# Expert stage of an encoder layer: TensorE in source order, residual ahead of the scatter, norm vectors in expert 14

## The chip, the cores and the metric

The kernel runs on one core of a Trainium2 chip. The metric is the device time of one execution in microseconds, the median of several runs. The engines of the core work side by side: TensorE (PE, matmuls), VectorE (DVE), ScalarE (ACT), GpSimd (POOL) and SyncE (SP), which issues the DMAs here.

## The reference, cut to what matters

```python
h = layer_norm(ALPHA * h + mix, ln1_g, ln1_b)           # 512 tokens x 1024; before it: attention and convolution
affinity = softmax(h @ w_router)                        # 16 experts
gates, idx = top_k(affinity.T, 64)                      # each expert picks its 64 best tokens
xg = h[idx]                                             # gather
a, u = xg @ w_gate[e], xg @ w_up[e]                     # 64x1024 by 1024x2048, for each expert e
y = (silu(a) * u) @ w_down[e] * gates                   # 64x2048 by 2048x1024
moe = zeros(512, 1024).at[idx].add(y)                   # scatter
out = layer_norm(ALPHA * h + moe, ln2_g, ln2_b)
```

All is float32. Each expert has three matrices of 8 MB, 403 MB for all 16; they are read once.

## The kernel before

**Stages.** Up to about 277 us the layer's first half runs (projections, attention, convolution, first norm, router, ranks of the first two experts). Then comes the expert stage, a loop over e = 0 to 15, two experts to a pair. An expert is a gate half (k = 0), an up half (k = 1), four steps j each, and a down part of eight chunks c. A step (k, j) reads one 2 MB transfer: two chunks of 128 rows by 2048 columns. In it run four inner steps (x, y): x is the chunk, y the 512-column bank, and each makes two matmuls, g = 0 and 1, on 64 of the 128 columns of TensorE. The trace shows every float32 matmul as two records, so an inner step is four records, a step (k, j) sixteen.

**Weights.** `stream` (L128) issues the next transfer on SP into the buffer at the front of `ring`, ten buffers `b0` to `b9` of 2 MB, and puts that buffer at the back; `take_big` takes one out for other use (for good with `back=False`). 22 chunks are fetched ahead, into the buffers under their other names `s_...` and a few small tiles. `stream` is called once behind each step (k, j) and each second down chunk, so a transfer can start when TensorE has read the buffer's last content.

**What rides along.** `ranks(e + 2)` (L1136): per token block a transpose of affinities, compares on VectorE (`mask`, L240), counts on TensorE (L245). `gather` (L1029): for each block of 128 columns four matmuls (L1044) and a ScalarE copy into `xg`, in expert 0 between the gate matmuls, for later pairs in the down part of each odd expert. `choice` (L1049): transposes and gates of the pair. `scatter` (L1083): for each token block t and half h two matmuls into one of two PSUM banks `sg`, from where the result goes into the sums `acc`; it runs in the up half of each even expert and, `alone`, in expert 15. `norm_rows` (L1116): the second norm of all rows without expert 15's. `spread` (L1006): turns a vector of 1024 numbers, kept as columns, into equal rows on all 128 partitions, by transposes and ScalarE copies.

**The residual.** `acc` takes a buffer in expert 2. The scatter of pair 0 writes it by a copy (L1097, L1099), the later ones add (L1095). `residual_pieces` (L1015), called from expert 3's first step on, takes a second buffer for a while; GpSimd makes eight pieces of alpha*h1 there, two operations each (L1024, L1025), and VectorE adds each to `acc` (L1027). The vectors of the second norm, `gb2`, are spread in expert 15, in the middle of its gate and up halves.

**What sets the order.** A scheduler orders the instructions of each engine by its own simulated times, but where the source calls `tc.keep_in_program_order`. The helper `tensor(...)` (L211) does that for a matmul as long as TensorE is in the set `ordered`; before, the expert stage calls `nc.tensor` directly and nothing there is pinned. Each engine runs its own instructions strictly in order. The gate and up results stand in `pgu`, one two-bank PSUM tile for each half:

```python
pgu = [ps.tile([128, 2, 512], F32, name=f"gu{k}") for k in range(2)]
...
nc.vector.tensor_tensor(hh[:, x], sg[:, x], p[:, x], op=OP.mult)   # behind the last up step, x = 0 and 1
...
nc.scalar.activation(sg, pgu[0], AF.Silu)                          # behind the last gate step
```

Of the kernel before, what the change touches and what calls it, by code (L numbers as in the profile page):

```python
# [46 lines left out]
def layer_kernel(ctx, tc, x, positions, emb_ln_g, emb_ln_b, w_in, q_norm_g, w_qb, kv_norm_g, w_kvb,  # L47
                 conv_w, conv_b, conv_ln_g, conv_ln_b, w_o, ln1_g, ln1_b, w_router,
                 w_gate, w_up, w_down, ln2_g, ln2_b, rope_rows, out):
    nc = tc.nc  # L50
# [949 lines left out]

    acc = []
# [4 lines left out]
    def spread(dst, c0, scale):  # L1006

        for q in range(2):
            p = ps.tile([128, 512], F32, name="sg", bufs=2)
            for c in range(4):  # L1010
                cc = c0 + 4 * q + c
                nc.tensor.transpose(p[:, c * 128:(c + 1) * 128], gb[:, cc:cc + 1].to_broadcast([128, 128]), ident)
# [36 lines left out]
    def choice(pair):  # L1049
# [9 lines left out]
        for x, src in enumerate((oh, turned)):  # L1059
            p = ps.tile([128, 512], F32, name="sg", bufs=2)  # L1060
            for t in range(TT):
                nc.tensor.transpose(p[:, t * 128:(t + 1) * 128], src[:, t], ident)
            g.append(quarter_tile(x, F32R))
            nc.scalar.activation(g[x], p, AF.Identity)
            for t in range(TT):
                nc.tensor.matmul(pg[:, 2 * x:2 * x + 2], src[:, t], aff[:, t, 2 * pair:2 * pair + 2],  # L1066
                                 start=t == 0, stop=t == TT - 1)
# [15 lines left out]
    def scatter(pair, alone):  # L1083

        g, _ = chosen.pop(pair)
        for t in range(TT):
            pp = [ps.tile([128, 512], F32, name="sg", bufs=2) for _ in range(2)]
            ts = slice(t * 128, (t + 1) * 128)
            for k, h in [(k, h) for k in range(2) for h in range(2)] if alone else [(k, h) for h in range(2) for k in range(2)]:
                rs = slice(h * 64, (h + 1) * 64) if alone else slice(0, 128)  # L1090
                nc.tensor.matmul(pp[h], g[h][rs, ts], parts[h][k][rs, :], start=k == 0, stop=k == 1)  # L1091
# [11 lines left out]
    def last_rows():  # L1103
# [3 lines left out]
        for hf in range(2):  # L1107
            for t in range(TT):
                nc.tensor.matmul(p[hf * 64:(hf + 1) * 64, :2], hot[E // 2 - 1][:, t, CAP:], ag[:, t],
                                 start=t == 0, stop=t == TT - 1)  # L1110
# [47 lines left out]
    for e in range(E):  # L1158
        pair, s = divmod(e, 2)
        last = e == E - 1  # L1160
        pgu = [ps.tile([128, 2, 512], F32, name=f"gu{k}") for k in range(2)]
# [14 lines left out]
        for k, j in order:  # L1176
# [4 lines left out]
            if last and (k, j) == (1, 0):  # L1181

                py = ps.tile([128, 512], F32, name="py")
                for t in range(TT):
                    for hf in range(2):
                        nc.tensor.matmul(py[hf * 64:(hf + 1) * 64], hot[E // 2 - 1][:, t, CAP:],
                                         acc[t][:, hf * 512:(hf + 1) * 512], start=t == 0, stop=False)
# [150 lines left out]
```

## Time and profile before

| what | us |
|---|---|
| median of 3 runs | 1203.52 (1202.52 to 1205.8) |
| profiled execution | 1208.29 |
| its span, first to last instruction | 1206.3 |
| TensorE busy (matmuls) | 1119.5 |
| VectorE, ScalarE, GpSimd busy | 400.4, 249.6, 203.2 |

The queues moved 422.85 MB in the span. Busy time is summed over the span; a record's time is from its start to its modelled end, so matmuls that run two at a time count once in the sum and each in the mean. The granted clock of TensorE is 1.00 (2.4 GHz) in nearly all of the expert stage.

### The profile page before, as it was taken

Reading aid. Unit: us, or ns where it says so; the run is one execution under the profiler, and the core shown is the slowest. Engines: PE = TensorE matmul, PEld = TensorE weight load, DVE = VectorE, ACT = ScalarE, POOL = GpSimd, SP = SyncE. Lnnn points to the kernel's source line nnn. Section 1 sums busy time; section 2 is a strip of 40 time slices with the busy share of each in tenths; the row PEclk is TensorE's granted clock in tenths of the full one; section 3 lists DMA queues with packets and bytes.
Section 4 is the critical chain, followed back from the end, with each engine's and each line's share of the span. In section 5 each row is a group of like instructions: output and inputs, shape, how many; then the busy total and the mean of one; then the engine's idle time right before and its main releaser. Section 6 shows DMA issues by size and latency. Waiting matters only on the chain.

```text
span 1206.3 us, 13663 instructions
## 1 busy us (share of the span) xinstructions
PE 1119.5 (93%) x5573; PEld 545.0 (45%) x5573; DVE 400.4 (33%) x905; ACT 249.6 (21%) x448; POOL 203.2 (17%) x234
## 2 busy tenths in 40 slices
PE   5899998999999998999999999999998998899996
PEld 3687776785334343433343334334332433243432
DVE  6799898543011115122021112011210122011252
ACT  4546677321111111101010011001000101010120
POOL 6778467210000007000000000000000000000041
PEclk9899899999999999999999999999999999999999
DMA  6421014777999998999999999999999999999996
GB/s 200 135 84 36 6 71 144 271 268 281 420 429 428 428 393 343 427 430 427 426 427 428 428 426 430 427 426 429 426 428 429 426 428 426 429 426 427 428 427 253
DMA packets 43681, 422.85 MB, mean 351 GB/s; under 512 B 5178, under 2 KB 13187, under 8 KB 18018
## 3 DMA queue, kind: packets, MB, share of 16 engines
q1 hardware_dynamic: 42032, 421.28, 84.3%
q8 instruction: 44, 0.72, 0.2%
q10 hardware_dynamic: 1506, 0.43, 0.2%
q0 software_dynamic: 80, 0.26, 0.1%
q14 instruction: 19, 0.16, 0.0%
HBM read 419.60 MB, written 2.36 MB: 350 GB/s over the span
## 4 chain that ended last, share of the span: by engine, by line
PE 73%; DMA 16%; DVE 6%; ACT 2%; issue 1%; POOL 1%; POOLq 0%; SPq 0%; ACTq 0%; DVEq 0%
PE gu L1199 30%; PE py L1276 16%; DMA b<-in_w_up_dram 6%; PE sg L1044 5%; DMA b<-in_w_down_dram 4%; PE pj L258 4%; PE pj L259 3%; PE pj L260 3%; DMA b<-in_w_gate_dram 3%; PE sg L1091 3%; PE st L772 1%; DVE sq L1210 1%; PE tr L1066 1%; DVE cv L453 1%; DMA s<-in_w_in_dram 1%
## 5 line engine op out<-in xcount | busy, mean ns | idle before, releaser
L1199 PE MATMUL gu<-b,xg 128*64 128x512 f32 x1920 | 439.1, 598 | 22.1 <-DVE sq L1210 10.9
L1199 PEld LDWEIGHTS gu<-b,xg 128*64 128x64 f32 x1920 | 133.8, 137 | 291.1 <-issue 244.5
L1276 PE MATMUL py<-b,sq 128*64 128x512 f32 x976 | 224.1, 598 | 0.0
L1056 POOL COPY sq<-oh 128x256 f32<-128x256 f32 x16 | 5.9, 400 | 799.4 <-PE sg L1250 799.4
L1210 DVE TENSOR_TENSOR sq<-sq,gu 128x512 f32<-128x512 f32 x30 | 20.6, 687 | 292.6 <-PE gu L1199 276.8
L1276 PEld LDWEIGHTS py<-b,sq 128*64 128x64 f32 x976 | 67.3, 136 | 109.4 <-issue 102.2
L258 PE MATMUL pj<-s,s 128*128 128x512 f32 x189 | 78.4, 424 | 7.6 <-ACT q L435 3.2
L1044 PE MATMUL sg<-oh,h 128*128 128x128 f32 x512 | 72.6, 290 | 8.3 <-DVE oh L1035 6.9
L1045 ACT ACTIVATE xg<-sg,gbp 128x128 f32<-128x128 f32 x64 | 29.3, 457 | 237.6 <-PE sg L1044 145.9
L1044 PEld LDWEIGHTS sg<-oh,h 128*128 128x128 f32 x512 | 64.6, 198 | 29.6 <-issue 21.6
L259 PE MATMUL pj<-s,s 128*128 128x512 f32 x189 | 77.1, 408 | 0.0
L228 POOL TENSOR_TENSOR s<-s,s 128x512 fp32r<-128x512 f32 (+2 forms) x54 | 64.8, 1223 | 19.0 <-ACT s L227 12.2
L240 DVE SCALAR_TENSOR_TENSOR mask<-tr,aff,ones_b 128x128 bf16<-128x128 f32 x84 | 26.1, 348 | 120.7 <-PE tr L238 120.7
L260 PE MATMUL pj<-s,s 128*128 128x512 f32 x157 | 63.2, 406 | 0.0
L453 DVE SCALAR_TENSOR_TENSOR cv<-s,q,cv 128x512 f32<-128x512 f32 x83 | 62.2, 749 | 1.7
L1212 ACT ACTIVATE sq<-gu 128x1024 f32<-128x1024 f32 x16 | 16.4, 1024 | 217.9 <-PE gu L1199 217.9
L1095 DVE TENSOR_TENSOR b<-sg,b 128x512 f32<-128x512 f32 x56 | 37.0, 687 | 58.3 <-PE sg L1091 58.3
L1091 PE MATMUL sg<-q,q 128*128 128x512 f32 (+1 forms) x128 | 42.2, 437 | 7.0 <-DVE b L1095 5.9
L1080 ACT ACTIVATE q<-py,gates 64x512 fp32r<-64x512 f32 x30 | 20.5, 682 | 131.7 <-PE py L1276 119.0
L258 PEld LDWEIGHTS pj<-s,s 128*128 128x128 f32 x189 | 37.5, 200 | 16.8 <-ACT q L435 3.7
L1081 DVE SCALAR_TENSOR_TENSOR q<-py,gates,q 64x512 fp32r<-64x512 f32 x30 | 22.5, 748 | 65.2 <-ACT q L1080 65.0
L259 PEld LDWEIGHTS pj<-s,s 128*128 128x128 f32 x189 | 37.4, 198 | 7.1
(288 smaller groups left out, 1112.8 us busy)
## 6 DMA issues: line engine op xcount, KB each, us to landing
b<-in_w_down_dram SPq DMA_DIRECT2D x60, 2048.0 KB, 25.8
b<-in_w_gate_dram SPq DMA_DIRECT2D x60, 2048.0 KB, 27.5
b<-in_w_up_dram SPq DMA_DIRECT2D x60, 2048.0 KB, 28.0
s<-in_w_gate_dram SPq DMA_DIRECT2D x8, 1024.0 KB, 6.8
s<-in_w_in_dram SPq DMA_DIRECT2D x12, 512.0 KB, 5.2
s<-in_w_up_dram SPq DMA_DIRECT2D x6, 1024.0 KB, 7.1
s<-in_w_down_dram SPq DMA_DIRECT2D x6, 1024.0 KB, 11.6
s<-in_w_o_dram SPq DMA_DIRECT2D x4, 1024.0 KB, 7.1
```

The costliest lines, as they stand in the source:

```text
L228: pin(eng, eng.tensor_tensor(lo, src, hi.bitcast(F32), op=OP.subtract))
L258: tensor(nc.tensor.matmul(p, a[0], b[0], start=start, stop=False, **kw))
L259: tensor(nc.tensor.matmul(p, a[0], b[1], start=False, stop=False, **kw))
L260: tensor(nc.tensor.matmul(p, a[1], b[0], start=False, stop=stop, **kw))
L453: nc.vector.scalar_tensor_tensor(part if k < CW - 1 else cva[j], src[k], w[k], cva[j] if k == n_act else part, op0=OP.mult, op1=OP.add)
L1044: nc.tensor.matmul(here, rows, oh[:, t, :], start=t == 0, stop=t == TT - 1)
L1045: nc.scalar.activation(xg[:, cc, :], here, AF.Identity, scale=gbp[:, 0, cc:cc + 1], bias=gbp[:, 1, cc:cc + 1])
L1091: nc.tensor.matmul(pp[h], g[h][rs, ts], parts[h][k][rs, :], start=k == 0, stop=k == 1)
L1095: nc.vector.tensor_tensor(a, pp[h], a, op=OP.add)
L1199: nc.tensor.matmul(p[g * 64:(g + 1) * 64, b, :], xg[:, c, s * CAP:(s + 1) * CAP], ws[a][2 * b + g], start=c == 0, stop=c == DC - 1)
L1210: nc.vector.tensor_tensor(hh[:, x], sg[:, x], p[:, x], op=OP.mult)
L1276: nc.tensor.matmul(py[x * 64:(x + 1) * 64, :], hT2[:, b, j, g * 64:(g + 1) * 64], w[2 * a + hf], start=f == 0 and not last, stop=f == 15)
```

## The change

1. TensorE joins `ordered` ahead of the expert stage and every matmul and transpose there goes through `tensor(...)`: its order is that of the source.
2. The rank steps stand behind every second inner step (`y` is 1) of the gate half, the last expert's scatter likewise.
3. `pgu` is four one-bank tiles; Silu is two operations.
4. `acc` is taken one step earlier, behind (2, 0, 0), the residual's buffer behind (2, 0, 1) in place of (3, 0, 0). GpSimd writes the residual straight into `acc`; every scatter, pair 0's too, adds to it. VectorE's eight adds (L1027) go.
5. `gb2` takes its buffer behind step (14, 0, 0), for good, and its spreads stand behind (14, 0, 0) and (14, 0, 1).

```diff
@@ ahead of the expert stage
+    ordered.add(nc.tensor)
     acc = []
@@ residual_pieces
         for a in range(2):
             spread(gb_l[a], a * DC, ALPHA)
+            yield
         for i in range(2 * TT):
             t, cs = i // 2, slice(i % 2 * 512, (i % 2 + 1) * 512)
-            r = t4[:, 2048 + i % 4 * 512:2048 + (i % 4 + 1) * 512]
+            r = acc[t][:, cs]
             nc.gpsimd.tensor_tensor(r, h1[:, t, cs], gb_l[0][:, cs], op=OP.mult)
             nc.gpsimd.tensor_tensor(r, r, gb_l[1][:, cs], op=OP.add)
-            yield
-            nc.vector.tensor_tensor(acc[t][:, cs], acc[t][:, cs], r, op=OP.add)
@@ gather, and likewise every other matmul and transpose of the stage
-                    nc.tensor.matmul(here, rows, oh[:, t, :], start=t == 0, stop=t == TT - 1)
+                    tensor(nc.tensor.matmul(here, rows, oh[:, t, :], start=t == 0, stop=t == TT - 1))
@@ scatter
                 if k == 1:
                     a = acc[t][:, h * 512:(h + 1) * 512]
-                    if pair:
-                        nc.vector.tensor_tensor(a, pp[h], a, op=OP.add)
-                    elif h:
-                        nc.vector.tensor_copy(a, pp[h])
-                    else:
-                        nc.scalar.activation(a, pp[h], AF.Identity)
+                    nc.vector.tensor_tensor(a, pp[h], a, op=OP.add)
@@ loop over the experts
-        pgu = [ps.tile([128, 2, 512], F32, name=f"gu{k}") for k in range(2)]
+        pgu = [[ps.tile([128, 512], F32, name=f"gu{k}{b}") for b in range(2)] for k in range(2)]
...
-                    if (k == 0) == last and not final and left > (0 if last else 1):
+                    if last:
+                        if k == 0 and y and left:
+                            step(sc)
+                            left -= 1
+                    elif k and not final and left > 1:
                         step(sc)
                         left -= 1
-                    elif k == 0:
+                    elif k == 0 and y:
                         step(rk)
...
-                nc.scalar.activation(sg, pgu[0], AF.Silu)
-            if residual is not None:
+                for b in range(2):
+                    nc.scalar.activation(sg[:, b], pgu[0][b], AF.Silu)
+            if (e, k, j) == (2, 0, 2):
                 step(residual)
                 step(residual)
             if last and (k, j) == (0, DC // 2 - 1):
-                gb2 = take_big()
...
                 nr = norm_rows()
...
-                if (e, k, j) == (2, 0, 2):
+                if (e, k, j) == (2, 0, 0):
                     t4 = take_big(back=False)
                     acc.extend(t4[:, t * D:(t + 1) * D] for t in range(TT))
-                elif (e, k, j) == (3, 0, 0):
+                elif (e, k, j) == (2, 0, 1):
                     residual = residual_pieces()
                     step(residual)
+                elif (e, k, j) == (E - 2, 0, 0):
+                    gb2 = take_big(back=False)
+                    g2, b2 = gb2[:, :D], gb2[:, D:2 * D]
+                    gb2h = quarters(gb2[:, 2 * D:])[:2]
+                    spread(g2, 2 * DC, 1.0)
+                elif (e, k, j) == (E - 2, 0, 1):
+                    spread(b2, 3 * DC, 1.0)
...
+                    stream(next_chunk[0] + 2)
```

TensorE at the end of expert 0, before. `s_...`, `sq` and `q_...` hold expert 0's weights, `b_...` expert 1's; `gu_2456` and `gu_2457` are expert 0's gate and up, `gu_2705` expert 1's gate.

```order
L1199 MATMUL gu_2456<-s_2420,xg 64x512 x4
L1199 MATMUL gu_2457<-sq,xg 64x512
L1199 MATMUL gu_2457<-q_2437,xg 64x512
L1199 MATMUL gu_2457<-q_2438,xg 64x512
L1199 MATMUL gu_2705<-b_2513,xg 64x512 x8
L1199 MATMUL gu_2705<-b_2541,xg 64x512 x5
L1199 MATMUL gu_2457<-sq,xg 64x512 x2
L1199 MATMUL gu_2457<-q_2439,xg 64x512
L1199 MATMUL gu_2457<-q_2440,xg 64x512
L1250 MATMUL tr<-ident,sq 128x128 x4
L1199 MATMUL gu_2705<-b_2541,xg 64x512 x3
L1199 MATMUL gu_2705<-b_2551,xg 64x512 x8
```

The same place after (`gu_2456` to `gu_2459` are expert 0's four banks):

```order
L1044 MATMUL sg<-oh,h_88 128x128 x4
L1194 MATMUL gu_2456<-s_2420,xg 64x512 x2
L1194 MATMUL gu_2457<-s_2420,xg 64x512 x2
L1194 MATMUL gu_2458<-sq,xg 64x512 x2
L1194 MATMUL gu_2458<-q_2437,xg 64x512
L1194 MATMUL gu_2458<-q_2438,xg 64x512
L1194 MATMUL gu_2459<-sq,xg 64x512 x2
L1194 MATMUL gu_2459<-q_2439,xg 64x512
L1194 MATMUL gu_2459<-q_2440,xg 64x512
L1253 MATMUL tr<-ident,sq 128x128 x4
L1253 MATMUL sg<-ident,sq 128x128 x4
L1279 MATMUL py<-s_2422,sq 64x512 x4
```

Expert 1's gate matmuls no longer stand among expert 0's; each gate pair stands right behind the gather of its column block, and the down matmuls (`py`) follow at once.

The queue of SP in expert 2 and 3, after. `b4` is the buffer that the residual's vectors were in (`b3` is `acc`):

```order
L157 DMA b5_2584<-in_w_down_dram 128x4096
L157 DMA b6_2607<-in_w_down_dram 128x4096
L157 DMA b7_2660<-in_w_gate_dram 128x4096
L157 DMA b4_2574<-in_w_up_dram 128x4096
L157 DMA b8_2681<-in_w_gate_dram 128x4096
L157 DMA b9_2693<-in_w_gate_dram 128x4096
```

In the ring `b4` stands behind `b2`; the scheduler has put its transfer ahead of that into `b8`.

The end of the queue of SP, before:

```order
L157 DMA b7_2657<-in_w_down_dram 128x4096
L157 DMA b8_2678<-in_w_down_dram 128x4096
L155 DMA b0_2503<-in_w_down_dram 128x1024 x4
L1133 DMA out_0_dram<-h1_88 128x1024 x4
```

And after (the last pair goes in four pieces in both):

```order
L157 DMA b8_2681<-in_w_down_dram 128x4096
L1128 DMA out_0_dram<-h1_88 128x1024
L157 DMA b9_2693<-in_w_down_dram 128x4096
L157 DMA b0_2489<-in_w_down_dram 128x4096
L1128 DMA out_0_dram<-h1_88 128x1024
L155 DMA b1_2499<-in_w_down_dram 128x1024 x4
L1128 DMA out_0_dram<-h1_88 128x1024 x2
```

Two of the four output transfers have moved ahead of the last down pairs.

## Rows read from the trace of the kernel before

**Rows 1.** The page: busy us, share, count; GB/s in 40 slices of 30.2 us.
```profile
PE 1119.5 (93%) x5573; PEld 545.0 (45%) x5573; DVE 400.4 (33%) x905; ACT 249.6 (21%) x448; POOL 203.2 (17%) x234
...
GB/s 200 135 84 36 6 71 144 271 268 281 420 429 428 428 393 343 427 430 427 426 427 428 428 426 430 427 426 429 426 428 429 426 428 426 429 426 427 428 427 253
```

**Rows 2.** Windows: busy us of each engine, granted clock, DMA share, GB/s.
```profile
290.00:330.00 40.00, 39.74 (x198) 15.83 (x194) 2.88 (x12) 4.73 (x7) 0.00 (x0) 1.00 0.99 415
420.00:485.00 65.00, 61.46 (x296) 23.83 (x294) 21.93 (x39) 7.54 (x12) 22.84 (x18) 0.97 0.93 371
485.00:950.00 465.00, 438.49 (x2200) 178.54 (x2198) 82.59 (x265) 45.71 (x77) 2.97 (x8) 1.00 1.01 428
950.00:1190.00 240.00, 223.45 (x1072) 88.65 (x1070) 56.79 (x107) 28.55 (x45) 16.74 (x16) 1.00 1.01 427
```

**Rows 3.** DMA issues of 490:560, then of 850:1150: count, KB, us to landing.
```profile
b<-in_w_gate_dram SPq DMA_DIRECT2D x4, 2048.0 KB, 17.6
...
b<-in_w_gate_dram SPq DMA_DIRECT2D x20, 2048.0 KB, 39.3
```

**Rows 4.** Time line, queue of SP: start us, us, what; two single issues.
```profile
288.48 0.33 SPq L157 DMA_DIRECT2D b<-in_w_down_dram  x1
...
319.42 0.33 SPq L157 DMA_DIRECT2D b<-in_w_down_dram  x1
```

**Rows 5.** Time line, TensorE, expert 0: start us, us, what, matmul records.
```profile
278.22 2.15 PE L1044 MATMUL sg<-oh,h 128*128 128x128 f32 x16 [0.26 <-DVE oh L1035]
...
324.27 6.23 PE L1199 MATMUL gu<-b,xg 128*64 128x512 f32 x28
```

**Rows 6.** Chain of work, two stretches: start us, us, what.
```profile
619.50 0.47 ACT xg L1045
...
621.22 3.58 PE py L1276 x16
...
624.81 0.26 PE tr L245 x7
...
663.91 0.98 PE tr L1066 x8
...
666.76 0.59 PE sg L1062 x4
```

**Rows 7.** Time line, GpSimd, then VectorE, while the residual is made.
```profile
454.55 5.02 POOL L1024 TENSOR_TENSOR b<-h,b 128x512 f32<-128x512 f32 x4 [20.41 <-ACT q L1080]
...
465.09 3.45 POOL L1024 TENSOR_TENSOR b<-h,b 128x512 f32<-128x512 f32 x2 [0.63 <-DVE both L249]
...
472.05 5.84 POOL L1025 TENSOR_TENSOR b<-b 128x512 f32<-128x512 f32 x4
...
454.56 0.76 DVE L1081 SCALAR_TENSOR_TENSOR q<-py,gates,q 64x512 fp32r<-64x512 f32 x1 [1.54 <-ACT q L1080]
...
461.43 3.58 DVE L1027 TENSOR_TENSOR b<-b,b 128x512 f32<-128x512 f32 x1
```

**Rows 8.** Chain of work, then TensorE, in the last expert.
```profile
1101.73 36.06 DMA b<-in_w_gate_dram
...
1149.79 37.42 DMA b<-in_w_down_dram
...
1184.01 13.95 PE L1276 MATMUL py<-b,sq 128*64 128x512 f32 x64
```

**Rows 9.** TensorE by line, 1137 to 1206: count, busy us, mean ns.
```profile
L1091 PE MATMUL sg<-q,q 64*128 64x512 f32 x16 | 5.1, 444 | 0.8 <-DVE b L1095 0.8
...
L1012 PE MATMUL sg<-ident,gb 128*128 128x128 f32 x16 | 2.4, 282 | 0.0
```

**Rows 10.** Waits: engine, line, whom; us in total, times, longest.
```profile
PE gu L1199 <- DVE sq L1210: 10.9, 13, 0.9
...
PE tr L245 <- DVE mask L240: 7.2, 7, 1.3
...
PE sg L1091 <- DVE b L1095: 5.9, 13, 0.8
```

More of the change, by code (lines that the diff above doesn't have):

```diff
@@ L1065, in choice @@
             for t in range(TT):
-                nc.tensor.matmul(pg[:, 2 * x:2 * x + 2], src[:, t], aff[:, t, 2 * pair:2 * pair + 2],
-                                 start=t == 0, stop=t == TT - 1)
+                tensor(nc.tensor.matmul(pg[:, 2 * x:2 * x + 2], src[:, t], aff[:, t, 2 * pair:2 * pair + 2],
+                                 start=t == 0, stop=t == TT - 1))
             yield
@@ L1090, in scatter @@
                 rs = slice(h * 64, (h + 1) * 64) if alone else slice(0, 128)
[L1091 removed]
+                tensor(nc.tensor.matmul(pp[h], g[h][rs, ts], parts[h][k][rs, :], start=k == 0, stop=k == 1))
                 if k == 1:
                     a = acc[t][:, h * 512:(h + 1) * 512]
[L1094 to L1099 removed]
+                    nc.vector.tensor_tensor(a, pp[h], a, op=OP.add)
                     if h or not alone:
@@ L1108, in last_rows @@
             for t in range(TT):
-                nc.tensor.matmul(p[hf * 64:(hf + 1) * 64, :2], hot[E // 2 - 1][:, t, CAP:], ag[:, t],
-                                 start=t == 0, stop=t == TT - 1)
+                tensor(nc.tensor.matmul(p[hf * 64:(hf + 1) * 64, :2], hot[E // 2 - 1][:, t, CAP:], ag[:, t],
+                                 start=t == 0, stop=t == TT - 1))
         gi = wk.tile([128, 2], F32, name="gi", bufs=1)
@@ L1185, in layer_kernel @@
                     for hf in range(2):
-                        nc.tensor.matmul(py[hf * 64:(hf + 1) * 64], hot[E // 2 - 1][:, t, CAP:],
-                                         acc[t][:, hf * 512:(hf + 1) * 512], start=t == 0, stop=False)
+                        tensor(nc.tensor.matmul(py[hf * 64:(hf + 1) * 64], hot[E // 2 - 1][:, t, CAP:],
+                                         acc[t][:, hf * 512:(hf + 1) * 512], start=t == 0, stop=False))
             if (k, j) == (1, 2) and s and not last:
@@ L1216, in layer_kernel @@
             if last and (k, j) == (0, DC // 2 - 1):
-                gb2 = take_big()
-                g2, b2 = gb2[:, :D], gb2[:, D:2 * D]
-                spread(g2, 2 * DC, 1.0)
-                spread(b2, 3 * DC, 1.0)
-                gb2h = quarters(gb2[:, 2 * D:])[:2]
-                for dst, src in zip(gb2h, (g2, b2)):
-                    for hf in range(2):
-                        rs = slice(hf * 64, (hf + 1) * 64)
-                        nc.scalar.activation(dst[rs], src[rs, hf * 512:(hf + 1) * 512], AF.Identity)
                 nr = norm_rows()
-            elif k and not final:
+            elif last and k and not final:
                 step(nr)
@@ L1232, in layer_kernel @@
             if not LATE <= i < LATE + 2:
-                if (e, k, j) == (2, 0, 2):
+                if (e, k, j) == (2, 0, 0):
                     t4 = take_big(back=False)
                     acc.extend(t4[:, t * D:(t + 1) * D] for t in range(TT))
-                elif (e, k, j) == (3, 0, 0):
+                elif (e, k, j) == (2, 0, 1):
                     residual = residual_pieces()
                     step(residual)
+                elif (e, k, j) == (E - 2, 0, 0):
[5 more added lines that the diff above has]
+                    spread(b2, 3 * DC, 1.0)
+                    for dst, src in zip(gb2h, (g2, b2)):
+                        for hf in range(2):
+                            rs = slice(hf * 64, (hf + 1) * 64)
+                            nc.scalar.activation(dst[rs], src[rs, hf * 512:(hf + 1) * 512], AF.Identity)
+                    stream(next_chunk[0] + 2)
                 else:
@@ L1275, in layer_kernel @@
                     hf = x if last else x ^ s
-                    nc.tensor.matmul(py[x * 64:(x + 1) * 64, :], hT2[:, b, j, g * 64:(g + 1) * 64],
-                                     w[2 * a + hf], start=f == 0 and not last, stop=f == 15)
+                    tensor(nc.tensor.matmul(py[x * 64:(x + 1) * 64, :], hT2[:, b, j, g * 64:(g + 1) * 64],
+                                     w[2 * a + hf], start=f == 0 and not last, stop=f == 15))
             if c % 2:
@@ L1294, in layer_kernel @@
     pm = ps.tile([128, 512], F32, name="tr")
-    nc.tensor.matmul(pm[:, :2], halves, mv[:, 0:2], start=True, stop=True)
+    tensor(nc.tensor.matmul(pm[:, :2], halves, mv[:, 0:2], start=True, stop=True))
     nc.vector.tensor_copy(mv[:, 3:4], pm[:, 0:1])
```

14 lines of the change are left out of this document (7 added, 7 removed).

## The prediction

> **What bounds the kernel now.** I read the 40 slices of the page first [rows 1]. TensorE is busy 93% of the span, but from slice 10 on the queues also move some 428 GB/s, slice after slice, with one dent, 393 and 343, in slices 14 and 15. Two things look full, so the question is which of them waits. The windows [rows 2] make the dent a number. In 485 to 950 and 950 to 1190 us the rate is 428 and 427, in 420 to 485 it is 371, in 290 to 330 it is 415. Then the time from issue to landing of one 2 MB transfer [rows 3]: 17.6 us at 490 to 560, 39.3 us at 850 to 1150. Transfers lie longer and longer in the queue, since TensorE frees buffers faster than the queue fills them. At 428 GB/s a transfer takes 4.90 us, so at the end eight of them stand in line. The last expert cannot begin before its first gate pair has landed, issued at 1101.73 and 36.06 us under way [rows 8]. So the weight stream is the bound from 485 us to its end, and the time can change in three ways only: the stream starts at another time, it runs empty for more or less, or less work is left behind its last byte. What TensorE saves in experts 4 to 13 goes into a longer queue and is worth nothing.
>
> **The start of the stream.** The first reuse of a buffer is issued at 288.48 [rows 4], when TensorE has finished the first gate pair. Now TensorE runs in source order: gather one column block (1.05 us, half of a row of 16 that took 2.15 [rows 5]), wait for ScalarE (0.47 us and two hand-overs, 0.53 [rows 6]), four matmuls (1.79, half of a 3.58 [rows 6]), a rank step, and the same again. From the first gather at 278.22 [rows 5] that is 2 x (1.05 + 0.53 + 1.79) and 0.3 to 0.6 of rank work: done at 285.5 to 285.8. Term one is -2.8 us.
>
> **The first expert.** In the old order TensorE ran the gate matmuls of expert 1 (28 of them at 324.27 [rows 5]) before expert 0's down matmuls, which freed buffers 1 to 3 early: the eighth reuse was issued at 319.42 [rows 4]. Pinned, the eighth reuse waits for expert 0's first down pair. Its time: 278.2, eight gathers with their wait 12.6, eight gate and up pairs 28.6, rank steps 1.7 (an estimate from [rows 6], where seven count matmuls take 0.26), Silu, product and transposes 1.5, then the first down pair with one round of expert turning and gates (3.58 + 0.5 + 1.0, [rows 6]): 327.7. Seven transfers are 34.3 us. Counting 2 us from an issue to the first packet (288.48 is issued and the queue is at speed some 2 us later), they run from 287.7, stand empty for 1.4, 0.8 and 0.5 us where a gathered gate pair comes late, and end at 324.7. The eighth begins at 329.7: 5.0 us empty. With smaller gaps of 0.6 the queue is empty for 8.3 us in this expert. Before, 40 us at 415 of 428 are 1.2 us, of which 0.5 lie before the first packet. Term two is +7.6 us. It rests on TensorE's own serial work, so I give it 2 us either way.
>
> **Experts 1 to 3.** Expert 1 costs TensorE 54.2 us (28.6 + 14.3 of matmuls, 8.4 of gathers, 1.7 of ranks, 1.2 of turning), so expert 2 begins at 394.1. Expert 2 skips two streams running (one for acc, one for the residual's vectors), and two of ten buffers are away. The queue's 23 transfers end at 408.2, the next is issued at 407.6 and starts at 409.6: 1.4 us empty, then 0.3. The next after that goes into the vectors' own buffer, which the order of SP puts ahead of buffer 8, so it waits for the last of GpSimd's 16 pieces, with everything on SP behind it. They start at 403.8, behind the first spread. A piece takes 1.255 us (four in 5.02 [rows 7]), so 16 take 20.1: the buffer is free at 423.9, the transfer starts at 426.0, 1.4 us empty. That makes 3.1. Before, 65 us at 371 of 428 [rows 2] are 8.7 us empty, in the stretch in which the scatter of expert 2 ran one buffer short and the residual's pieces then held a second one. Term three is -5.6 us. GpSimd writes the four left halves before the four right ones, so the scatter's fourth piece waits until about 420.9 for its PSUM bank and TensorE stands 3 us; the hidden cover is the transfer just named, which keeps the queue fed until 430.9, while buffer 8 comes free at 427.2.
>
> The price of a piece is the open one. No row is cheaper. From above: 1.46 where VectorE's two-SBUF adds ran beside it (four in 5.84) and 1.73 (two in 3.45 [rows 7]). I take 1.255, since the scatter's add reads one operand from PSUM, and the nearest such row, line 1081 at 454.56, took its usual 0.76 inside GpSimd's run, while line 1027, with both operands in SBUF, took 3.58 [rows 7]. On this the Trainium skill (SBUF — State Buffer, Who interferes with whom) has a rule: a VectorE instruction with at most one SBUF input does not contend with GpSimd, one with two does, and the second to issue is blocked outright. The trace agrees on both kinds; by the rule the piece stays at its price, and no run here shows the add itself beside it.
>
> **The end.** The third down pair of expert 15 lands at 1187.2 (issued 1149.79, 37.42 under way), and the four quarters of the last follow it by 4.9 us: 1192.1. TensorE, however, ends its down matmuls only at 1198.0 (13.95 us from 1184.01, gapless [rows 8]); the least it needs after the last quarter is 0.9. It is 4.9 us behind. Out of expert 15 go two spreads (2.4 us [rows 9]), the wait for VectorE between the halves of the up bank (0.84, 13 of them make 10.9 [rows 10]) and waits on the scatter's adds, so TensorE waits for each pair and the lag goes: -4.9 us. But the norms are now ready early, and SP issues two of the four output rows ahead of the last two down pairs. Each is 512 KB, 1.2 us of the queue: +2.4. Taking a buffer for the norms in expert 14 costs nothing while seven transfers stand in line. Term four is -2.5 us. Behind TensorE's end the same 8.3 us follow.
>
> **The sum.** -2.8 + 7.6 - 5.6 - 2.5 = -3.3 us. The profiled execution took 1208.29 us for its span of 1206.3, the median of the runs is 1203.52; the sum is made on the span and I carry it to the median: 1200.2 us. Within 0.3% (3.6 us, about what a measurement of this kernel can tell from no change) that is no change, but only just.
>
> **The rivals.** *GpSimd holds SP* (slower). SP is blocked behind the vectors' buffer. If a piece costs 1.73, the 16 take 27.7 us, the buffer comes at 431.5, and the queue is empty for 7.6 us more: 1207.8. From 1.46 a piece the whole gain is gone, from about 1.68 it is a loss that can be told. For it speaks that VectorE's adds run all through that stretch, against it line 1081. *The first expert loses less* (faster). The gap of 5 us depends on the eighth reuse; if gathers overlap more than the chain of waits shows, it halves, and with the earlier start stays: 1196.5. *The tail keeps its lag.* If TensorE does not catch up in expert 15 (its scatter alone is 5.1 us [rows 9], and the matmuls on the sums stand in the way too), the end moves with the stream only: -0.8, 1202.7. *TensorE is the bound.* Then every removed wait counts, 10.9 us behind the products, 7.2 behind the rank masks, 5.9 behind the scatter's adds [rows 10]: 24 us, 1179.5. Against it stand landing times that grow and a rate that doesn't move. The Trainium skill (Perfetto Trace Analysis, Identifying the Most-Contended Engine) says that a matmul's busy share is no good measure of TensorE's closeness to its limit; the 93% of the page agrees with that reading. *The pin or the spacing doesn't act*: the order of the built program shows both, so I give it nothing.
>
> **How the numbers follow.** Forecast 0.50 (1197.5 to 1203, from 2 us on term two and 1 us on the others), GpSimd holds SP 0.17 (1203.5 to 1209), first expert loses less 0.15 (1195 to 1198), tail keeps its lag 0.14 (1201 to 1204.5), TensorE the bound 0.04. The range 1195.5 to 1206.5 leaves out the last and most of the second's upper half. Faster by over 0.3% is below 1199.9: 0.45 of the forecast, all of the third and the last, 0.41. Slower is above 1207.1: 0.5 of the second and a little of the rest, 0.11. The same: 0.48.
>
> **What would show it.** In the profile after: the first L157 issue near 285.7; an empty stretch near 325 to 330; the windows of 420 to 485 at 400 GB/s or more; SP's wait for GpSimd ending near 424; the rate at 428 from 435 on; TensorE waiting for w_down pairs in expert 15, with less than 1.5 us between the last landing and its end. It is wrong if GpSimd's pieces take over 1.4 us, if the gap in the first expert is under 3 or over 8 us, or if TensorE in expert 15 runs without a wait.

## The result, and the profile after

The changed kernel takes 1216.11 us, median of 5 runs (1213.91 to 1217.95), against 1204.8 us of 5 runs of the kernel before beside it: a ratio of 1.0094 with a 95% interval of 1.0073 to 1.0115. It is 11.3 us slower, where 3.3 us faster had been forecast, and outside the range. The profiled execution took 1214.44 us for a span of 1212.4.

The page of the changed kernel (busy us and share; GB/s in 40 slices of 30.3 us) answers [rows 1]:

```profile
PE 1120.7 (92%) x5573; PEld 532.5 (44%) x5573; DVE 382.5 (32%) x901; ACT 250.2 (21%) x460; POOL 199.1 (16%) x234
...
GB/s 199 135 86 37 3 71 194 282 267 272 306 421 428 315 398 428 429 426 428 428 427 427 428 425 430 428 428 427 426 429 426 428 429 425 429 425 428 428 427 277
```

The dent of [rows 1], 393 and 343 in slices 14 and 15, is now 315 and 398 in slices 13 and 14 (counted from 0), and slice 10 has fallen from 420 to 306. The windows (busy us of TensorE, its weight loads, VectorE, ScalarE and GpSimd, then granted clock, DMA share, GB/s) answer [rows 2]:

```profile
290.00:330.00 40.00, 34.79 (x185) 15.45 (x183) 4.48 (x19) 5.85 (x10) 0.75 (x2) 1.00 0.79 307
330.00:420.00 90.00, 84.05 (x428) 33.64 (x426) 12.72 (x53) 11.54 (x21) 8.02 (x7) 1.00 0.93 386
420.00:485.00 65.00, 60.91 (x288) 21.83 (x286) 13.17 (x37) 4.96 (x9) 12.55 (x12) 1.00 0.99 410
485.00:950.00 465.00, 441.18 (x2152) 170.43 (x2150) 80.91 (x256) 44.71 (x80) 2.99 (x8) 1.00 1.01 427
```

Of the kernel before, [rows 2] lacks one of these stretches:

```profile
330.00:420.00 90.00, 88.75 (x438) 35.79 (x436) 14.62 (x56) 11.42 (x19) 0.74 (x2) 1.00 1.01 428
```

From 485 us on nothing has changed, 427 GB/s against 428. What is lost is lost ahead of that: 307 and 386 GB/s where there were 415 and 428, and 410 in place of 371 gives only a part back. The granted clock is 1.00 throughout. TensorE is busy for 34.79 of the first 40 us, against 39.74 before, although the weights it reads there had long been fetched: it waits for something else. Of these 5.2 us, 2.7 are waits for the copies behind the gathers (5 waits), which the prediction counted; 2.3 are new. The time line of TensorE in the gate half of expert 2 (start us, us, what, records, in brackets the idle time ahead and who ended it) shows for what:

```profile
400.55 0.32 PE L238 MATMUL tr<-ident,aff 128*128 128x128 f32 x1
400.80 1.94 PE L1194 MATMUL gu<-b,xg 128*64 128x512 f32 x8
402.67 0.32 PE L238 MATMUL tr<-ident,aff 128*128 128x128 f32 x1
403.71 0.16 PE L245 MATMUL tr<-ones_b,mask 128*128 128x1 bf16 x1 [0.72 <-DVE mask L240]
403.81 1.94 PE L1194 MATMUL gu<-b,xg 128*64 128x512 f32 x8
405.67 0.32 PE L238 MATMUL tr<-ident,aff 128*128 128x128 f32 x1
406.99 0.19 PE L245 MATMUL tr<-ones_b,mask 128*128 128x1 bf16 x2 [0.99 <-DVE mask L240]
407.11 1.94 PE L1194 MATMUL gu<-b,xg 128*64 128x512 f32 x8
408.98 0.32 PE L238 MATMUL tr<-ident,aff 128*128 128x128 f32 x1
410.56 0.21 PE L245 MATMUL tr<-ones_b,mask 128*128 128x1 bf16 x3 [1.26 <-DVE mask L240]
410.64 1.07 PE L1013 MATMUL sg<-ident,gb 128*128 128x128 f32 x8
```

And VectorE at the first two of these steps (the same columns):

```profile
400.91 0.35 DVE L240 SCALAR_TENSOR_TENSOR mask<-tr,aff,before 128x128 bf16<-128x128 f32 x1 [0.50 <-PE tr L238]
...
403.03 0.35 DVE L240 SCALAR_TENSOR_TENSOR mask<-tr,aff,ones_b 128x128 bf16<-128x128 f32 x1 [0.97 <-PE tr L238]
...
403.30 0.35 DVE L240 SCALAR_TENSOR_TENSOR mask<-tr,aff,before 128x128 bf16<-128x128 f32 x1
```

A rank step is a transpose of block t, its compares on VectorE, and then the count of block t - 1. The mask that the count at 403.71 reads was made at 400.91. It waits for the two compares of the next block, which have just been let go by the transpose ahead of it: 0.72, 0.99 and 1.26 us, 2.97 us in an expert. The mask itself is not what it waits for: its load as weights runs at 402.67, 0.15 us, ahead of the wait. The source shows what is left: the compares read one part of the tile `tr`, the count writes another part, and the order of the source is kept for the tile as a whole. That this is the reason is read from the source; no run here gives the counts a tile of their own. The list of waits has the sum for 14 experts (us in total, times, longest):

```profile
PE tr L245 <- DVE mask L240: 41.7, 42, 1.3
```

In [rows 10] the same wait was 7.2 us, 7 times. The other two waits of that group are all but gone: none behind the products, 1.1 us at the scatter. On SP the three issues on which the prediction's steps rest (the first, the eighth and the 24th reuse of a buffer) answer [rows 4]:

```profile
282.31 0.33 SPq L157 DMA_DIRECT2D b<-in_w_down_dram  x1
...
329.15 0.33 SPq L157 DMA_DIRECT2D b<-in_w_up_dram  x1
...
415.67 0.33 SPq L157 DMA_DIRECT2D b<-in_w_down_dram  x1
```

The first gather stands at 274.87 in this trace and at 278.22 in [rows 5]; in the 14 profiles of this study it stands between 273.9 and 278.6, although the source ahead of it is the same. So I count from it: the eighth is issued 54.3 us behind it (forecast 49.5), the 24th 140.8 (forecast 129.4).

### The profile page after: what moved, and what is told of

It is laid out like the page before. It is cut to its first block, busy times and chain, and to the rows that moved or that the text cites. A ratio compares the mean times of both kernels' runs of the same rounds, so it can differ in the third digit from the quotient of the medians.

```text
span 1212.4 us, 13661 instructions
## 1 busy us (share of the span) xinstructions
PE 1120.7 (92%) x5573; PEld 532.5 (44%) x5573; DVE 382.5 (32%) x901; ACT 250.2 (21%) x460; POOL 199.1 (16%) x234
## 4 chain that ended last, share of the span: by engine, by line
PE 79%; DVE 7%; DMA 6%; ACT 3%; POOL 2%; issue 2%; POOLq 0%; SPq 0%; ACTq 0%; DVEq 0%
PE gu L1194 35%; PE py L1279 18%; PE sg L1044 6%; PE pj L258 3%; DVE mask L240 3%; PE pj L259 3%; PE pj L260 3%; PE sg L1091 3%; DMA b<-in_w_down_dram 3%; DVE cv L453 1%; PE tr L238 1%; ACT s L227 1%; DMA out_dram<-h 1%; PE tr L1066 1%; PE st L772 1%
## 5 line engine op out<-in xcount | busy, mean ns | idle before, releaser
L1194 PEld LDWEIGHTS gu<-b,xg 128*64 128x64 f32 x1920 | 127.4, 136 | 240.6 <-issue 235.7
L1279 PE MATMUL py<-b,sq 128*64 128x512 f32 x976 | 227.3, 600 | 3.4 <-DMA b<-in_w_down_dram 3.4
L1279 PEld LDWEIGHTS py<-b,sq 128*64 128x64 f32 x976 | 63.2, 136 | 106.6 <-issue 94.6
L258 PE MATMUL pj<-s,s 128*128 128x512 f32 x189 | 77.0, 416 | 7.7 <-ACT q L435 3.2
L1044 PE MATMUL sg<-oh,h 128*128 128x128 f32 x512 | 76.5, 292 | 0.7 <-DVE oh L1035 0.7
L259 PE MATMUL pj<-s,s 128*128 128x512 f32 x189 | 76.2, 403 | 0.0
L1094 DVE TENSOR_TENSOR b<-sg,b 128x512 f32<-128x512 f32 x64 | 43.8, 690 | 101.1 <-PE sg L1091 88.9
L260 PE MATMUL pj<-s,s 128*128 128x512 f32 x157 | 62.0, 398 | 0.0
L1257 ACT ACTIVATE sq<-tr 128x512 f32<-128x512 f32 x16 | 9.6, 597 | 253.4 <-PE tr L1253 253.4
L1212 ACT ACTIVATE sq<-gu 128x512 f32<-128x512 f32 x32 | 18.9, 597 | 205.6 <-PE gu L1194 205.6
L245 PE MATMUL tr<-ones_b,mask 128*128 128x1 bf16 x140 | 11.4, 165 | 41.7 <-DVE mask L240 41.7
L258 PEld LDWEIGHTS pj<-s,s 128*128 128x128 f32 x189 | 36.7, 195 | 16.5 <-ACT q L435 3.7
## 6 DMA issues: line engine op xcount, KB each, us to landing
s<-in_w_down_dram SPq DMA_DIRECT2D x6, 1024.0 KB, 11.3
```

Source lines behind the costliest of these rows:

```text
L258: tensor(nc.tensor.matmul(p, a[0], b[0], start=start, stop=False, **kw))
L259: tensor(nc.tensor.matmul(p, a[0], b[1], start=False, stop=False, **kw))
L260: tensor(nc.tensor.matmul(p, a[1], b[0], start=False, stop=stop, **kw))
L1044: tensor(nc.tensor.matmul(here, rows, oh[:, t, :], start=t == 0, stop=t == TT - 1))
L1194: tensor(nc.tensor.matmul(p[b][g * 64:(g + 1) * 64, :], xg[:, c, s * CAP:(s + 1) * CAP], ws[a][2 * b + g], start=c == 0, stop=c == DC - 1))
L1279: tensor(nc.tensor.matmul(py[x * 64:(x + 1) * 64, :], hT2[:, b, j, g * 64:(g + 1) * 64], w[2 * a + hf], start=f == 0 and not last, stop=f ...
```

## The experiments

Two times from each trace sort the kernels: from the first gather to the landing of the 37th reused buffer (the last that comes more than 0.3 us late in the kernel before), and from there to the end of the span. The ratios are to runs of the kernel before that were taken beside each kernel. Where the text gives the queue's empty time, it is an estimate made as in the prediction: 4.90 us a transfer, 2 us from an issue to the first packet.

| kernel | to the 37th landing | from there to the end | median, us | ratio to before, 95% interval |
|---|---|---|---|---|
| before | 204.1 | 724.0 | 1204.8 | |
| after | 216.1 | 721.5 | 1216.11 | 1.0094 (1.0073 to 1.0115) |
| e1, counts first | 205.5 | 721.4 | 1206.73 | 1.0015 (0.9999 to 1.0031) |
| e10, counts first in experts 0 to 2 | 206.1 | 721.3 | 1203.98 | 0.9985 (0.9970 to 1.0001) |
| e11, counts first in 3 to 13 | 217.7 | 721.2 | 1218.43 | 1.0098 (1.0069 to 1.0128) |
| e2, no pin | 201.2 | 721.2 | 1199.95 | 0.9958 (0.9941 to 0.9974) |
| e4, counts first, pin from expert 1 | 200.7 | 721.5 | 1200.2 | 0.9951 (0.9936 to 0.9966) |
| e5, e4 and rows late | 200.5 | 720.1 | 1199.63 | 0.9950 (0.9931 to 0.9968) |
| e12, e5 and ranks of expert 2 later | 197.9 | 720.0 | 1197.77 | 0.9932 (0.9907 to 0.9957) |
| e6, residual alone | 206.1 | 724.0 | 1208.77 | 1.0017 (1.0003 to 1.0031) |
| e7, norm vectors alone | 204.2 | 722.8 | 1205.21 | 0.9984 (0.9968 to 0.9999) |
| e8, banks and spacing alone | 207.8 | 722.8 | 1211.22 | 1.0041 (1.0021 to 1.0061) |
| e9, pin and spacing alone | 217.8 | 732.8 | 1227.41 | 1.0179 (1.0151 to 1.0206) |
| e3, pin alone | 222.3 | 759.9 | 1261.77 | 1.0470 (1.0445 to 1.0495) |

**The counts first.** The changed kernel with one exchange:

```diff
+            if t:
+                count(t - 1, pr[:, 256:256 + TT], ms[t - 1])
             if t < TT:
                 ms.append(mask_tile(wk, 2))
                 compare(e, t, pr[:, t % 2 * 128:(t % 2 + 1) * 128], ms[t])
-            if t:
-                count(t - 1, pr[:, 256:256 + TT], ms[t - 1])
```

> The changed kernel with one exchange in the rank steps: the counts of the block before stand ahead of the next block's transpose and compares. Theory A: pinned in the old order, each count waits for a compare it doesn't need (41.7 us in all, about 3 us in each expert), and the three stops in experts 0, 1 and 2 make the weight stream run empty there. Then TensorE's wait at the counts falls from 41.7 to under 5 us, the empty time of expert 0 falls from 12.7 to about 8 to 9 us, that of expert 2 from 9.6 to about 3 to 4, and the time is 1205 to 1207 against 1216.1. Rival B: the source order as such is late in the first experts and the waits at the counts only fill time that TensorE would spend waiting elsewhere: the wait goes, but the time stays at 1213 to 1216.

Theory A held. The time line of TensorE in expert 2 of this kernel:

```profile
395.14 0.32 PE L238 MATMUL tr<-ident,aff 128*128 128x128 f32 x1
395.39 1.94 PE L1194 MATMUL gu<-b,xg 128*64 128x512 f32 x8
397.26 0.18 PE L245 MATMUL tr<-ones_b,mask 128*128 128x1 bf16 x1
397.30 0.30 PE L238 MATMUL tr<-ident,aff 128*128 128x128 f32 x1
397.53 1.94 PE L1194 MATMUL gu<-b,xg 128*64 128x512 f32 x8
```

And two of its windows, with the columns of [rows 2]:

```profile
290.00:330.00 40.00, 37.05 (x201) 16.69 (x197) 4.49 (x19) 6.40 (x11) 0.74 (x2) 1.00 0.86 333
330.00:420.00 90.00, 88.91 (x442) 34.28 (x441) 14.80 (x56) 11.59 (x22) 16.89 (x14) 1.00 1.00 416
```

The count at 397.26 starts with the end of the matmuls ahead of it; no count waits any more. The 24th reuse is issued 130.4 us behind the first gather in place of 140.8, that is 10.4 us earlier, of which three experts' waits are 8.9. The rest goes with the waits too. From the start of a step to the matmul behind it TensorE takes 1.14, 1.44 and 1.66 us in the changed kernel (402.67 to 403.81, 405.67 to 407.11, 408.98 to 410.64) and 0.27, 0.30 and 0.23 in e1, where the step overlaps the matmuls around it: 3.44 us an expert, 10.3 in three. The median falls by 9.4 us.

The kernel before had an order of this kind in the experts that count. TensorE in its expert 0:

```profile
285.29 0.18 PE L245 MATMUL tr<-ones_b,mask 128*128 128x1 bf16 x1
285.33 0.30 PE L238 MATMUL tr<-ident,aff 128*128 128x128 f32 x1
```

The count stands right ahead of a transpose and waits for nothing. The scheduler had put it there, and the pin took that away.

**Where a wait counts.** The same exchange for the first three experts alone, and for all but these (`ranks` is called two experts ahead). Against e1:

```diff
-            if t:
+            if t and e < 5:             # the other kernel: e >= 5
                 count(t - 1, ...)
...
+            if t and not e < 5:
+                count(t - 1, ...)
```

> The changed kernel with the counts first in experts 0, 1 and 2 alone; the waits in the eleven experts behind stay, some 32 us of them. Theory A: TensorE sets the time up to the 24th reused buffer, in expert 2, and the stream from there on; a wait counts in full ahead of that point and not at all behind it: 1205.5 to 1207.5, as with all of them gone. Rival B: every expert's waits count alike: 3 of 14 of the 9.4 us, 1213 to 1215.

> The changed kernel with the counts first in all experts but 0, 1 and 2: the mirror image. Theory A: nothing is gained, 1214.5 to 1217. Rival B: 11 of 14 of the 9.4 us, 1207 to 1210.

The wait at the counts in the first kernel (us in total, times, longest):

```profile
PE tr L245 <- DVE mask L240: 32.8, 33, 1.3
```

And in the second:

```profile
PE tr L245 <- DVE mask L240: 8.9, 9, 1.3
```

With 32.8 us of waits left the kernel is as fast as with none (1203.98, if anything under A's 1205.5); with 8.9 us left it is as slow as with all (1218.43, above A's 1217, but a ratio of 1.0098 against 1.0094). These waits count in full up to the 24th or 27th reused buffer, and those behind it, 32.8 us, not at all. Rival B, in which every expert's waits count alike, is out.

**Parts of the pin.** The changed kernel without the pin (the line `ordered.add(nc.tensor)` taken out):

> The changed kernel without the pin: TensorE's order is the scheduler's again, all other parts of the change stay. Theory A (the pin is what costs, by the counts and by the first expert's order): the stream starts 3 us later again, but runs empty for under 2 us in expert 0 and 3 to 5 us in experts 1 to 3; 1198 to 1202. Rival B (the early residual and the lost buffers in expert 2 are what costs): expert 2 still runs empty for some 9 us, 1203 to 1207.

And with the counts first and the pin from expert 1 on:

```diff
-    ordered.add(nc.tensor)
     acc = []
...
+        if e == 1:
+            ordered.add(nc.tensor)
         pair, s = divmod(e, 2)
```

> The changed kernel with the counts first and the pin only from expert 1 on. Theory A: the first reuse comes some 10 us behind the first gather again (7.3 with the pin), expert 0's gap ahead of the eighth reuse stays at 3 to 5 us, because expert 1's gate matmuls are still kept behind expert 0's down part; expert 2 about 3 us empty; 1199 to 1203. Rival B: the pin in expert 0 is not what opens the gap: as the run with the counts first, 1205 to 1207.

Both times came out in the range of A. In e2 the split is another: the queue is empty for 3.6 us in expert 0, where A said under 2, and for 2.1 behind it, where it said 3 to 5. With the pin from expert 1 on the first reuse is issued 10.3 us behind the first gather in place of 7.4, 2.9 us later, and the 24th all the same 5.0 us earlier than in e1 (125.4 against 130.4): TensorE is busy for 39.83 of the 40 us from 290 to 330, against 37.05 in e1. In expert 0 the scheduler finds work for the waits behind the gathers, which the source order leaves empty: 4.4 us in 8 waits of the gate matmuls in e1, no such row in e4. In one point A was wrong: the gap ahead of the eighth reuse is 0.7 us and not 3 to 5.

**One part at a time.** The kernel before with the pin alone:

> The kernel before with the pin alone, every other part of the change left out. Theory A: the waits at the counts appear here too (about 40 us in all), expert 0 runs empty for about 12 us, experts 1 to 3 for more than before (8.7), since the scatter and the residual stand where they stood and TensorE comes later: 1213 to 1220. Rival B (the residual and buffer part of the change costs, not the pin): 1203 to 1208.

The direction was right, the size was not: 1261.77. In e3 TensorE stays the bound behind the 37th landing too. The time line of TensorE at the start of the gate half of expert 7:

```profile
706.78 1.08 PE L1200 MATMUL gu<-b,xg 128*64 128x512 f32 x4
709.25 0.32 PE L238 MATMUL tr<-ident,aff 128*128 128x128 f32 x1 [1.39 <-DVE mask L240]
710.29 0.16 PE L245 MATMUL tr<-ones_b,mask 128*128 128x1 bf16 x1 [0.72 <-DVE mask L240]
710.39 1.08 PE L1200 MATMUL gu<-b,xg 128*64 128x512 f32 x4
...
712.72 0.19 PE L245 MATMUL tr<-ones_b,mask 128*128 128x1 bf16 x2 [0.99 <-DVE mask L240]
712.84 1.97 PE L1200 MATMUL gu<-b,xg 128*64 128x512 f32 x4
```

And three windows of that stretch:

```profile
705.00:712.80 7.80, 4.69 (x22) 1.21 (x18) 3.39 (x14) 1.36 (x2) 0.00 (x0) 0.96 1.00 426
712.80:718.00 5.20, 3.93 (x14) 0.94 (x13) 1.35 (x9) 0.00 (x0) 0.00 (x0) 0.50 0.98 394
718.00:725.00 7.00, 7.00 (x28) 2.25 (x28) 0.86 (x2) 0.00 (x0) 0.00 (x0) 0.69 0.70 257
```

The rank steps stand behind every inner step there, so the waits follow each other within 8 us. TensorE is busy for 4.69 of 7.80 us, then the granted clock falls to 0.50 (1.2 GHz), and four records take 1.97 us in place of 1.08. The clock stays there from 712.1 to 722.3, with TensorE busy for 8.32 of these 10.2 us. The 84th, 108th, 132nd and 156th reuse are issued 122.7 to 122.8 us apart, where 24 transfers of 4.90 us take 117.5. Of the 5.3 us too many the clock takes some 4.2, half of the 8.32 (an estimate); the rest I did not assign. The next kernel has the pin and the steps behind every second inner step (`elif k == 0 and y`; the last expert's scatter likewise), no other part:

> The kernel before with the pin and the rank steps behind every second inner step, nothing else. Theory A: in the run with the pin alone the counts' waits stand so close together that the granted clock falls to 0.50 for some 8 us in every second expert, and a pair of experts takes TensorE 122.8 us against 117.5 of the stream; spaced, the clock stays at 1.00, a pair takes under 118 us, and most of the loss against 1261.8 goes: 1217 to 1228. Rival B: the wait behind the products (13.0 us) is what makes TensorE the bound there: 1240 or more.

The windows of the same stretch in this kernel:

```profile
705.00:712.00 7.00, 4.99 (x24) 1.52 (x23) 1.79 (x11) 0.00 (x0) 0.00 (x0) 1.00 1.01 428
712.00:718.00 6.00, 5.03 (x29) 1.83 (x30) 1.94 (x11) 0.00 (x0) 0.00 (x0) 1.00 1.00 426
```

The clock stays at 1.00, and 34 us of the loss are gone (1227.41): A. The counts' waits themselves are nearly the same, 41.7 us against 43.7, so it isn't their sum that cost these 34 us. What is left behind the 37th landing (732.8 against 724.0) is TensorE's lag at the end: it runs its down matmuls there without a gap, as before (13.95 us from 1206.59), but further behind the last weights. The spacing, which the prediction gave no price, is worth that much as soon as the order is pinned; without the pin no run has it by itself (e8 has it beside the banks and is not faster).

The other three parts alone, on the kernel before:

> The kernel before with the residual part alone: acc taken one step earlier, the residual made in expert 2 straight in acc, every scatter adds. Theory A: the stream's empty time behind 400 us falls from 9.0 to about 3 us and nothing else changes: 1199 to 1201 against 1205.7. Rival B: the early residual is worth nothing and the gain of the run without the pin comes from the end of the kernel: 1204 to 1207.

> The kernel before with the norm vectors in expert 14 alone. Theory A: TensorE ends about 1 us behind the last weights in place of 5.9 us, less 2.4 us for two output rows that move ahead of the last down pairs: 2 to 3 us faster, 1202.5 to 1204. Rival B: the lag at the end comes from the waits in the up half and the scatter, not from the vectors: 1205 to 1208, with the two rows ahead as a loss.

> The kernel before with the four one-bank gate and up tiles and the rank steps behind every second inner step alone, no pin. Theory A (the weight stream is the bound): TensorE's wait behind the products (10.9 us) goes and buys nothing but at most 1 us at the end: 1204.5 to 1206.5. Rival B (TensorE is the bound): 10 us faster, 1195 to 1197.

The norm vectors give 1.5 us by the medians (1.9 by the ratio), under A's 2 to 3; it lies behind the 37th landing (724.0 to 722.8). By its time the run falls into B's range, but not by its trace. Its list of waits has for TensorE's down matmuls:

```profile
PE py L1280 <- DMA b<-in_w_down_dram: 0.4, 1, 0.4
```

Here TensorE waits for the last weights, where before 13.95 us ran without a gap: the lag goes with the vectors, as A said. The output rows that move ahead of the last weights take a part of it back (1.4 us in e4, by e5 below). The residual alone gives nothing (1208.77, above both ranges, a ratio of 1.0017): A's gain failed to come. The late transfers of 420 to 485 us go, but the 24th, now right behind the two buffers that are taken out, is issued 6.7 us too late, 130.1 us behind the first gather. The banks with the spacing take the wait behind the products away (10.9 us in [rows 10], no such row here) and are no faster: TensorE then waits 18.5 us for up weights and 5.1 for gate weights, against 8.8 and 1.4 before. B is out with it; but the kernel is 0.4% slower, which A did not say either. The scheduler's order came out another way, with 2.9 us of empty queue ahead of the eighth reuse and 6.4 ahead of the 37th. I did not follow that further.

**Towards a faster kernel.** As e4, with the output rows collected in a list and issued on SP behind the last weights (SP's order is pinned in expert 15 for it):

```diff
-            nc.sync.dma_start(out[0, t * 128:(t + 1) * 128, :], o)
+            rows_out.append((t, o))
             yield
...
             if c % 2:
                 stream(next_chunk[0] + 2)
+                if last:
+                    send_rows()
```

> As the run pinned from expert 1 on, with the four output rows issued behind the last weights. Theory A: the two rows that lay ahead of the last down pairs cost 2 x 1.2 us of the queue, and TensorE waits for the last weights there, so the end comes 2.4 us earlier: 1197 to 1198.5 against 1200.2. Rival B: the rows fill time the queue has over, or become the last thing themselves: 1200 to 1202.

And the same with the rank steps of expert 2 in its up half:

```diff
-                    elif k == 0 and y:
+                    elif k == 0 and y and e != 2:
+                        step(rk)
+                    if e == 2 and k and y:
                         step(rk)
```

> As the run with the rows late, with the rank steps of expert 2 in its up half, behind the 24th reused buffer. Theory A: 1.9 us of TensorE's work move behind the point up to which it sets the time; the empty time of 2.8 us in expert 2 falls to about 1 us: 1197 to 1198.5 against 1199.6. Rival B: the buffers that come next (up half) are late by the same amount, and nothing is gained: 1199 to 1200.5.

In e5 the stretch behind the 37th landing is 1.4 us shorter, not 2.4; the medians (1199.63 and 1200.2) don't tell the two kernels apart, and 1199.63 lies between the ranges of A and B. TensorE's last down matmuls in e5 show where the other microsecond stays:

```profile
1179.04 7.09 PE L1288 MATMUL py<-b,sq 128*64 128x512 f32 x32 [1.33 <-DMA b<-in_w_down_dram]
```

From the landing of the third down pair TensorE needs 7.1 us for the two pairs left, and the last four quarters take only 4.9 to come. So the row ahead of the second pair counted with its 1.2 us, and the row behind the third pair did not. In e12 the 24th reuse comes 1.8 us earlier than in e5 and the 37th landing 2.6; 1197.77 us is in A's range, 0.68% faster than the kernel before, and the lowest median here. Its interval overlaps those of e2, e4 and e5, so by time alone it isn't told apart from them. Two of its windows show how little is left of the new dent:

```profile
290.00:330.00 40.00, 39.83 (x208) 17.95 (x206) 3.74 (x14) 5.99 (x10) 0.74 (x2) 1.00 0.99 406
330.00:420.00 90.00, 88.86 (x438) 34.36 (x435) 16.96 (x58) 11.55 (x21) 19.86 (x16) 1.00 1.00 425
```

## Why the prediction was wrong, point by point

**The bound.** That the weight stream is the bound from 485 us on is right; from there the rate is 427 or 428 GB/s up to 950 us in all kernels whose windows I read but e3 (417), and e10 and e11 show that waits of TensorE are free there. What the prediction did not draw from this is the other half: wherever the queue stands empty up to the 24th reuse, the stream waits for TensorE to free a buffer, so in experts 0 to 2 what TensorE loses is on the path. The Trainium skill (Perfetto Trace Analysis, Optimization Strategy) says that the most-contended engine can change in the course of a kernel, and that gaps are to be looked for on the engine of the regime in question. e10 and e11 agree, with 32.8 us of waits that cost nothing and 8.9 that cost 10 to 12 (216.1 against 206.1, 217.7 against 205.5).

**The start of the stream.** Right: the first reuse is issued 7.44 us behind the first gather, against 10.26, and -2.8 had been forecast (the terms of its sum give 285.3 to 285.6, some 0.2 less than the 285.5 to 285.8 that it states). As a gain it was none: e4 starts 2.9 us later than e1 and has its 37th landing 4.8 us earlier. An early start only lengthens the next gap when TensorE decides when that gap ends.

**The first expert.** This is the step that failed: "rank steps 1.7 (an estimate from [rows 6], where seven count matmuls take 0.26)". It prices the instructions and not the waits that the pin puts between them. They are 2.97 us in each expert, on top, and with the overlap that is lost 3.44. The issues on SP, at 4.90 us a transfer, leave 12.6 us empty in this expert where 8.3 had been forecast; with the waits gone (e1) 9.1, and the eighth reuse 50.8 us behind the first gather (forecast 49.5). So the rest of the term holds to 1.3 us, the gap of 5 us ahead of the eighth (5.28) included.

**Experts 1 to 3.** The same estimate is in "1.7 of ranks" of expert 1, and once more in expert 2. The 24th reuse was forecast 129.4 us behind the first gather and is at 140.8; in e1 it is at 130.4. The queue is empty for 9.6 us, forecast 3.1, in e1 2.8. The GpSimd part of this step is right. Time line of GpSimd and of VectorE while the residual is made, which answers [rows 7]:

```profile
411.98 9.96 POOL L1026 TENSOR_TENSOR b<-h,b 128x512 f32<-128x512 f32 x8 [87.17 <-ACT b L1014]
421.90 9.91 POOL L1027 TENSOR_TENSOR b<-b,b 128x512 f32<-128x512 f32 x8
...
423.21 0.69 DVE L1094 TENSOR_TENSOR b<-sg,b 128x512 f32<-128x512 f32 x1 [9.25 <-POOL b L1027]
425.20 0.69 DVE L1094 TENSOR_TENSOR b<-sg,b 128x512 f32<-128x512 f32 x1 [1.30 <-PE sg L1091]
```

Sixteen pieces take 19.9 us (forecast 20.1), and VectorE's adds beside them take the 0.69 us that they take elsewhere. The Trainium skill (SBUF — State Buffer, Who interferes with whom) says that a VectorE instruction with at most one input in SBUF, outside the two-port modes, does not contend with GpSimd; the trace agrees, for an add that no row of before showed. The rival *GpSimd holds SP* is out with it: SP waits 5.3 us for the last piece, and the transfer behind it starts 0.8 us late.

**The end.** Right in its sum: from the 37th landing to the end it is 724.0 us before and 721.5 after, -2.5 as forecast. The end of TensorE's time line answers [rows 8]:

```profile
1186.24 3.65 PE L1279 MATMUL py<-b,sq 128*64 128x512 f32 x16
1191.96 3.65 PE L1279 MATMUL py<-b,sq 128*64 128x512 f32 x16 [2.06 <-DMA b<-in_w_down_dram]
1196.94 7.19 PE L1279 MATMUL py<-b,sq 128*64 128x512 f32 x32 [1.32 <-DMA b<-in_w_down_dram]
```

TensorE now waits for each down pair, as the prediction asked for, where it ran 13.95 us without a gap. By single edits the parts are other than forecast: the vectors, with the rows that move ahead, give 1.2 us (e7), banks and spacing 1.2 (e8), and the two rows ahead of the last weights cost the end 1.4 and not 2.4 (e5 against e4). Without the rows TensorE would still end some 2.2 us behind the last weights (7.1 less 4.9, an estimate from e5), where 0.9 had been forecast: the lag was worth about 1 us less than its term and the rows cost 1 us less than theirs. That the two cancel is luck. The rival *the tail keeps its lag* is out.

**The sum.** Counted from the first gather, the steps forecast -0.8 us up to the 37th landing and -2.5 behind it; measured are +12.0 and -2.5. With the counts first it is +1.4 and -2.6. The whole error but about 2 us is one term, the rank steps, of which those of three experts count. What the 2 us are isn't settled; 1.0 is in the 24th reuse, and two short gaps behind it (0.7 and 0.8 us) make 1.2 more than forecast. The prediction's own signs of being wrong stayed silent: GpSimd's pieces take 1.24 us (the sign was over 1.4), the gap in the first expert is 5.28 (under 3 or over 8), and TensorE waits in expert 15. No sign watched the gap ahead of the 24th reuse, 8.1 us where 1.4 had been forecast.

**The rivals.** None of them had the mechanism. *TensorE is the bound* came nearest, with the wrong sign and in the wrong place: it took [rows 10], "7.2, 7, 1.3" behind the rank masks, for a wait that goes with the change. The row was the price of the one that comes. The scheduler had let a count wait 7 times, for up to 1.3 us, none of them in experts 0 to 2; there it had run the transposes further ahead and put a count right before the next one, as the lines at 285.29 show. The pinned order has the wait each time. A rival *slower* could have been worked out from it: up to 1.3 us a count, three counts an expert, three experts that matter, some 9 us.

## What to carry to other kernels

Before an order is pinned, read in the source which instructions stand right behind what they wait for: a scheduler that was free to move them hides their price, and a wait that the trace shows a few times can be the price of every such pair, as here (7 times before, 42 after). Then find the last point at which the bounding queue stood empty: ahead of it what the engine that frees buffers loses counted in full here, and behind it not at all as long as that engine had slack left (in e3 it had none), so gains and losses that come ahead of it are not to be added up stretch by stretch, but read off as the time of that one issue.

## What the runs showed of the hardware

TensorE's granted clock fell to 0.50 (1.2 GHz) in e3 although no single wait in the stretch ahead was longer than 1.4 us; TensorE had been busy for 4.69 of 7.80 us there. It was back at 1.00 (2.4 GHz) in the window of 725 to 735. In e9, where it was busy for 4.99 of 7.00 us in the same stretch, it stayed at 1.00. The same fall, for 10.2 us each time, stands in five experts of e3, every second one from expert 5 on.

And a pin alone, with no other change in the source, cost 4.7%, two thirds of it (759.9 against 724.0) behind the point from which the stream had been the bound. That the stream was the bound there rested on slack of TensorE, which the waits at three counts and the lower clock in every second expert used up.
